# A decoder layer on one core: the ACT and Vector instructions of a transposed block in another order, and another start of the first product

## The chip, the cores and the metric

The kernel runs on one core of a Trainium2 chip. The metric is device time in microseconds (us) of one execution, with all loads and stores. Lower is better. In what follows PE is the tensor engine (matmuls and transposes), ACT the scalar engine, DVE the vector engine, SP the engine whose queue issues most DMAs.

## The reference, cut to what matters

One layer of a decoder over 256 tokens (two halves `m` of 128) with 2048 channels in float32: a normalised input goes through a wide product, two attention branches, an output product, an MLP with squared ReLU, and a gated embedding at the end.

```python
u = rmsnorm(h, g_mix_pre)                       # 256 x 2048
proj = u @ w_in                                 # 2048 x 10240: q, k, v of both branches, two gates
oa, ob = moba_attention(...), diff_attention(...)
mixed = sigmoid(ga) * (oa @ w_br_moba) + sigmoid(gb) * (ob @ w_br_diff)
h = h + rmsnorm(mixed @ w_out, g_mix_post)
u2 = rmsnorm(h, g_mlp_pre)
h = h + rmsnorm(square(relu(u2 @ w_up)) @ w_down, g_mlp_post)
gate = sigmoid(rmsnorm(h, g_ple_pre) @ w_ple_gate)
h = h + rmsnorm((p @ w_ple_proj) * gate, g_ple_post)
```

## The kernel before, in words

Every product is a row of chunks of 512 output columns (`Chunk`, `run`). A chunk of 16 k-tiles is done in 8 pieces `s` of two k-tiles (512 KB of weights), each for the two token halves `m`. A float32 product is built from three matmuls on halves of the numbers: weights are split into `whi` (an ACT copy, `head`, L227) and `wlo` (a DVE subtraction, `low`, L234), the moving side likewise into `hi` and `lo`. So one piece for one half is two times (L294 with `whi` and the high part of u, L295 with `wlo` and the high part, L296 with `whi` and the low part of u), six matmuls of 512 columns.

The order is written by hand: each engine runs its instructions in program order, and the waits between engines are put in by the layer that the kernel is written in, from what each instruction reads and writes. `ensure(i)` emits the splitting of weights up to piece `i`; `heads` and `low` feed ACT and DVE. Raw weights have 5 buffers, split ones 8. SP loads raw piece `i` when the DVE subtraction of piece `i - 5` is done.

Three times the left side of a product is made from rows in SBUF: u from x in the first product, u2 and u3 from h at two boundaries (after the output product, and after the last down product). A block is 128 tokens by 512 channels. `turn` (L173) makes four PE transposes into one PSUM bank; `turned` (L180) scales them by the norm's gain while copying them out: for each of four columns of 128, one ACT instruction writes the high part (L189) and one DVE instruction the low part (L190, it reads the same bank and the high part). With a gain there are 8 blocks at each of the three places, 24 in all, 96 pairs of instructions.

In the first product a hook, `first`, places that work: the x blocks of the next four k-tiles are transposed at the hook of `(s, 1)` for even `s`, ahead of that piece's matmuls, and `turned` at the hook of the next odd `s`. Before it stands the start (L613 to L637): DMAs, idle matmuls on zeros (`warm`), the gain's transpose, the first block and the first piece of weights, which is split in two halves of one k-tile.

At a boundary the class `Boundary` (L717) places, in a list, turns `T(m, kg)`, scalings `U(m, kg)`, the residual additions `A(m, kg)` on DVE (L746) that make h, and single weight splits `H(s)` on ACT and `L(s)` on DVE, among two short products (`pp_ch`) and the next product.

Of the kernel before, what the change touches and what calls it, by code (L numbers as in the profile page):

```python
# [11 lines left out]
F32 = mybir.dt.float32  # L12
F32R = mybir.dt.float32r
I32 = mybir.dt.int32
AF = mybir.ActivationFunctionType
ALU = mybir.AluOpType
# [3 lines left out]
P = 128  # L20
# [10 lines left out]
CW = 512  # L31
KT = 2
# [4 lines left out]
NB = 8  # L37
# [42 lines left out]
def tile_hybrid_block(ctx: ExitStack, tc: tile.TileContext, a, out: bass.AP):  # L80
    nc = tc.nc
    pe, act, dve = nc.tensor, nc.scalar, nc.vector
# [7 lines left out]
    wp = ctx.enter_context(tc.tile_pool(name="wp", bufs=1))  # L90
# [5 lines left out]
    def aux(name):  # L96
        return ps.tile([P, 512], F32, name=name, tag="aux", bufs=4)
# [5 lines left out]
    gT = [cst.tile([P, NT], F32, name=f"gT{i}") for i in range(3)]  # L103
# [7 lines left out]
    def load_small():  # L111
        for i, g in ((1, "g_mlp_pre"), (2, "g_ple_pre")):
            nc.sync.dma_start(gr[i], a[g][0].rearrange("(k p) -> k p", p=P))
        nc.sync.dma_start(con[:, P:C_END], a["consts"][:, P:C_END])
        for i, n in enumerate(("lambda_q1", "lambda_k1", "lambda_q2", "lambda_k2")):
            nc.sync.dma_start(lamv[:, i, :], a[n][0:1, :].to_broadcast([P, HD]))
        nc.sync.dma_start(gsub, a["diff_subln_g"][0:1, :].to_broadcast([P, 2 * HD]))

    def setup_gain(i):
        g_ps = aux("g_ps")  # L120
        pe.transpose(g_ps[:, 0:NT], gr[i], ident[0:NT, 0:NT])
        dve.tensor_copy(gT[i], g_ps[:, 0:NT])
# [14 lines left out]
    def rstd(ss, n, out_ap, tag, rest=None):  # L137


        w = ss.shape[-1]  # L140
        v = sm.tile([P, w], F32, name="v", tag=f"v{tag}", bufs=2)
        dve.tensor_scalar(v, ss, -0.5 / n, -0.5 * EPS if rest is None else rest, op0=ALU.mult, op1=ALU.add)
        y = sm.tile([P, w], F32, name="y", tag=f"y{tag}", bufs=2)
        dve.tensor_scalar(y.bitcast(I32), v.bitcast(I32), -0.5, 519526879.0, op0=ALU.mult, op1=ALU.add)
        t = sm.tile([P, w], F32, name="t", tag=f"t{tag}", bufs=2)
        for i in range(3):
            if w == 1:
                dve.tensor_scalar(t, v, y, y, op0=ALU.mult, op1=ALU.mult)
            else:
                dve.tensor_mul(t, y, y)  # L150
                dve.tensor_mul(t, t, v)
            dve.scalar_tensor_tensor(out_ap if i == 2 else y, t, 1.5, y, op0=ALU.add, op1=ALU.mult)
# [16 lines left out]
    def split(hi, lo, src):  # L169
        act.activation(hi, src, AF.Copy)  # L170
        dve.tensor_sub(lo, src, hi.bitcast(F32))

    def turn(src):  # L173

        t_ps = aux("t_ps")
        for j in range(4):
            pe.transpose(t_ps[:, j * P:(j + 1) * P], src[:, j * P:(j + 1) * P], ident)
        return t_ps.rearrange("p (j t) -> p j t", j=4)

    def turned(t_ps, dst, kg, m, gain=None, js=range(4)):  # L180

        s = slice(m * P, (m + 1) * P)
        if gain is None:
            split(dst.hi[kg][:, :, s], dst.lo[kg][:, :, s], t_ps)
            return
        for j in js:
            g = gT[gain][:, 4 * kg + j:4 * kg + j + 1]
            hi = dst.hi[kg][:, j, s]
            act.activation(hi, t_ps[:, j], AF.Copy, scale=g)  # L189
            dve.scalar_tensor_tensor(dst.lo[kg][:, j, s], t_ps[:, j], g, hi.bitcast(F32), op0=ALU.mult, op1=ALU.subtract)  # L190


    chunks = []
# [1 line left out]
    conv = {}  # L195
# [3 lines left out]
    raws = {}  # L199
# [12 lines left out]
    def loads(i):  # L212
        while state["load"] <= i:
            load(state["load"])

    def head(i):

        c, s = todo[i]
        kts = c.subs[s]
        n = len(kts)  # L220
        loads(i)
        raw = raws.pop(i)
        cuts = [slice(j, j + 1) for j in range(n)] if i < 2 else [slice(0, n)]
        hi = wp.tile([P, KT, CW], F32R, name="whi", tag="whi", bufs=NB)
        lo = wp.tile([P, KT, CW], F32R, name="wlo", tag="wlo", bufs=NB)
        for j in cuts:
            act.activation(hi[:, j], raw[:, j], AF.Copy)  # L227
        conv[i] = (hi, lo, raw, cuts)

    def low(i):  # L230

        hi, lo, raw, cuts = conv[i]
        for j in cuts:
            dve.tensor_sub(lo[:, j], raw[:, j], hi[:, j].bitcast(F32))  # L234
        conv[i] = (hi, lo)

    def heads(i):
        last = min(i, state["used"] + NB - 1, len(todo) - 1)
        while state["head"] <= last:
            head(state["head"])  # L240
            state["head"] += 1

    def ensure(i):
        last = min(i, state["used"] + NB - 1, len(todo) - 1)
        while state["conv"] <= last:
            heads(state["conv"])
            low(state["conv"])
            state["conv"] += 1
# [89 lines left out]
    uT = Tbuf("A", "u")  # L338
    oT = Tbuf("B", "o")
    x_sb = [gp.tile([P, 2, 2, CW], F32, name=f"x{i}", tag="xg", bufs=2) for i in range(2)]  # L340
# [43 lines left out]
    def attention(u):  # L384
# [101 lines left out]
        for m in range(2):  # L486
            t_ps = turn(ob[:, m].rearrange("p h d -> p (h d)"))
            yield
            turned(t_ps, oT, u, m)
# [24 lines left out]
    def mix(n):  # L514
        for _ in range(3):
            yield
        for m in range(2):
            t_ps = turn(G[n][:, 1, m, :])
            yield
            turned(t_ps, mT, n, m)  # L520

    all_kt = list(range(NT))
    c_in = []
# [6 lines left out]
    for tag, u, kind, col in seq:  # L530
# [4 lines left out]
        c = Chunk(w_in, all_kt, col, uT)  # L535
# [3 lines left out]
    for n in range(4):  # L539
        for wh in range(2):  # L540
            c = Chunk(w_in, all_kt, 6144 + 2048 * wh + n * CW, uT)
# [3 lines left out]
    for n in range(4):  # L545
        for wh in range(2):
            c = Chunk(w_bm if wh == 0 else w_bd, list(range(8)), n * CW, None)
# [37 lines left out]
    def load_x(kg):  # L585
        nc.sync.dma_start(x_sb[kg // 2][:, kg % 2], x_d[:, kg * CW:(kg + 1) * CW].rearrange("(m p) c -> p m c", p=P))

    xt = {}

    def first(s, m):  # L590
        kg = (s + 1) // 2
        if (s, m) == (0, 1):
            xt[1] = turn(x_sb[0][:, 0, 1])
            turned(xt[1], uT, 0, 1, 0)
        if s % 2 == 0:
            if m and kg < 3:
                xt.update({mm: turn(x_sb[(kg + 1) // 2][:, (kg + 1) % 2, mm]) for mm in range(2)})
            if m and kg < 2:
                load_x(kg + 2)
        elif kg < 4 and m == 0:  # L600
            for mm in range(2):
                turned(xt[mm], uT, kg, mm, 0)
        for k, mm in {3: ((0, m),), 5: ((1, m),), 6: ((2, m),), 7: ((3, 0), (3, 1)) if m == 0 else ()}.get(s, ()):
            junk = at.tile([P, CW], F32, name="junk", tag="t1", bufs=1)
            act.activation(junk, x_sb[k // 2][:, k % 2, mm], AF.Square, accum_out=ss1[:, mm, k:k + 1])
        if (s, m) == (5, 1):
            load_small()
        if (s, m) == (7, 0):
            ss1t = sm.tile([P, 2], F32, name="ss1t", bufs=1)
            dve.tensor_reduce(ss1t, ss1, AX.X, ALU.add)  # L610
            rstd(ss1t, D, rs1, "x")
# [4 lines left out]
    def warm(n):  # L616
        w = aux("warm")
        for i in range(n):
            pe.matmul(w[:, 0:P], lhsT=z, rhs=z, start=True, stop=True)
# [4 lines left out]
    nc.scalar.dma_start(x_sb[0][:, 0, 1], x_d[P:T, 0:CW])  # L624
    loads(2)
    load_x(1)
    warm(8)
    setup_gain(0)
    warm(2)
    xt[0] = turn(x_sb[0][:, 0, 0])  # L630
    head(0)
    turned(xt[0], uT, 0, 0, 0, range(2))
    low(0)
    turned(xt[0], uT, 0, 0, 0, range(2, 4))
    state["head"] = state["conv"] = 1
    c_in[0].hook = first
    c_in[0].ahead = lambda s, m: (2 * m, 2, 2, 2, 2, 2, 4, 5)[s]  # L637

    for c in order1:
# [242 lines left out]
    for g in range(4):  # L882
        hT = Tbuf("A", f"h{g}")
        for n in range(4):
            c = up_ch[4 * g + n]
# [13 lines left out]
        for n in range(4):  # L899
            c = dn_ch[g][n]  # L900
# [89 lines left out]
```

## Time and profile before

| | |
|---|---|
| median of 3 runs | 1524.48 us (1522.71 to 1524.62) |
| profiled execution: time, span | 1523.25 us, 1521.5 us |
| PE busy | 1488.4 us, 98% |
| DVE busy | 866.7 us, 57% |
| ACT busy | 716.5 us, 47% |
| DMA | 185 GB/s over the span, queue q1 57% of 16 engines |
| mean granted clock of PE | 0.99 of full |

The span is the time from the first to the last instruction; the 1.75 us beside it lie around it. Busy shares are means over stages with different limits. The rows below are from several views of the same execution: `idle before` and `<-` name the wait of an engine and what ended it.

### The profile page before, as it was taken

To read this page: it belongs to the slowest core of one execution; us is meant where nothing else is said; L and a number is where in the kernel's file an instruction comes from. 1 tells how busy PE (TensorE), PEld (TensorE's weight loads), DVE (VectorE), ACT (ScalarE), POOL (GpSimd) and SP (SyncE) were. 2 spreads that over 40 slices of the span, in tenths; PEclk is the share of its full clock that TensorE was granted. 3 is DMA by queue.
4 is the path that set the end of the run, shared out by engine and by line. 5 is a ranking of instruction groups with operands and counts; after the bars stand their busy time and mean duration, and the time that the engine had idled before them with its cause. 6 is when DMAs were issued, how large, how long until landed. Compare 5 with 4: busy or idle time off the path is not lost.

```text
span 1521.5 us, 18536 instructions
## 1 busy us (share of the span) xinstructions
PE 1488.4 (98%) x7119; PEld 1245.1 (82%) x7119; DVE 866.7 (57%) x1111; ACT 716.5 (47%) x995; POOL 0.2 (0%) x4
## 2 busy tenths in 40 slices
PE   8999999999999999998999999999999999999897
PEld 6788888888888888886888888888888888888686
DVE  4755555655344565556664456545655555655675
ACT  5654444554544444445554444433544344543662
POOL 0000000000000000000000000000000000000000
PEclk9999999999999999999999999999999999999999
DMA  7655555555466556744656564666456646565272
GB/s 228 222 188 163 182 157 177 167 177 183 153 221 207 180 187 221 250 138 149 211 180 201 187 207 157 208 204 194 156 190 217 194 149 214 182 205 201 68 247 94
DMA packets 146537, 282.14 MB, mean 185 GB/s; under 512 B 8928, under 2 KB 10896, under 8 KB 146192
## 3 DMA queue, kind: packets, MB, share of 16 engines
q1 hardware_dynamic: 145984, 280.28, 57.0%
q8 instruction: 56, 0.92, 0.2%
q10 hardware_dynamic: 464, 0.66, 0.1%
q14 instruction: 33, 0.27, 0.1%
HBM read 278.81 MB, written 2.10 MB: 185 GB/s over the span
## 4 chain that ended last, share of the span: by engine, by line
PE 91%; DVE 4%; ACT 3%; DMA 1%; issue 1%; SPq 0%; DVEq 0%; ACTq 0%
PE acc L295 22%; PE acc L296 22%; PE acc L294 22%; PE acct L322 15%; PE acct L323 7%; DVE u L190 2%; ACT u L189 2%; DVE wlo L234 1%; ACT whi L227 1%; DVE h L746 1%; PE s_ps L397 1%; DMA raw<-in_w_in 1%; PE acc L950 0%; PE acc L952 0%; PE acc L951 0%
## 5 line engine op out<-in xcount | busy, mean ns | idle before, releaser
L234 DVE TENSOR_TENSOR wlo<-raw,whi 128x1024 fp32r<-128x1024 f32 (+1 forms) x518 | 617.7, 1219 | 423.3 <-ACT whi L227 422.6
L227 ACT ACTIVATE whi<-raw 128x1024 fp32r<-128x1024 f32 (+1 forms) x518 | 531.4, 1051 | 406.6 <-PE acc L296 283.7
L322 PE MATMUL acct<-u,whi 128*128 128x512 f32 x960 | 338.4, 397 | 1.0 <-ACT r L827 1.0
L294 PE MATMUL acc<-whi,u 128*128 128x512 f32 x768 | 309.3, 403 | 5.5 <-ACT whi L227 4.8
L295 PE MATMUL acc<-wlo,u 128*128 128x512 f32 x768 | 302.6, 394 | 5.3 <-DVE wlo L234 5.3
L296 PE MATMUL acc<-whi,u 128*128 128x512 f32 x768 | 302.5, 394 | 0.0
L323 PE MATMUL acct<-u,wlo 128*128 128x256 f32 x960 | 269.4, 281 | 0.0
L322 PEld LDWEIGHTS acct<-u,whi 128*128 128x128 f32 x960 | 180.2, 188 | 45.2 <-ACT r L827 1.4
L295 PE MATMUL acc<-wlo,h 128*128 128x512 f32 x512 | 199.2, 389 | 0.0
L294 PE MATMUL acc<-whi,h 128*128 128x512 f32 x512 | 199.2, 389 | 0.0
L296 PE MATMUL acc<-whi,h 128*128 128x512 f32 x512 | 199.2, 389 | 0.0
L323 PEld LDWEIGHTS acct<-u,wlo 128*128 128x128 f32 x960 | 181.4, 189 | 0.2
L294 PEld LDWEIGHTS acc<-whi,u 128*128 128x128 f32 x768 | 146.3, 190 | 37.1 <-ACT whi L227 7.3
L295 PEld LDWEIGHTS acc<-wlo,u 128*128 128x128 f32 x768 | 146.0, 190 | 36.3 <-DVE wlo L234 7.5
L296 PEld LDWEIGHTS acc<-whi,u 128*128 128x128 f32 x768 | 145.8, 190 | 30.9
L294 PEld LDWEIGHTS acc<-whi,h 128*128 128x128 f32 x512 | 96.1, 188 | 20.1
L296 PEld LDWEIGHTS acc<-whi,h 128*128 128x128 f32 x512 | 96.1, 188 | 19.9
L295 PEld LDWEIGHTS acc<-wlo,h 128*128 128x128 f32 x512 | 96.1, 188 | 19.8
L844 ACT ACTIVATE r<-acct 128x256 f32<-128x256 f32 x60 | 22.8, 379 | 67.7 <-PE acct L323 67.7
L189 ACT ACTIVATE u<-t_ps,gT 128x128 fp32r<-128x128 f32 x96 | 34.0, 366 | 43.9 <-DVE u L190 42.4
L190 DVE SCALAR_TENSOR_TENSOR u<-t_ps,gT,u 128x128 fp32r<-128x128 f32 x96 | 32.8, 349 | 36.6 <-ACT u L189 36.6
L845 DVE TENSOR_TENSOR r<-acct,r 128x256 f32<-128x256 f32 x60 | 24.5, 422 | 47.2 <-ACT r L844 47.2
(160 smaller groups left out, 1041.4 us busy)
## 6 DMA issues: line engine op xcount, KB each, us to landing
raw<-in_w_in SPq DMA_DIRECT2D x159, 512.0 KB, 4.2
raw<-in_w_up SPq DMA_DIRECT2D x128, 512.0 KB, 4.2
raw<-in_w_down SPq DMA_DIRECT2D x128, 512.0 KB, 5.3
raw<-in_w_out SPq DMA_DIRECT2D x32, 512.0 KB, 5.2
raw<-in_w_ple_gate SPq DMA_DIRECT2D x32, 512.0 KB, 5.4
raw<-in_w_br_moba SPq DMA_DIRECT2D x16, 512.0 KB, 3.9
raw<-in_w_br_diff SPq DMA_DIRECT2D x16, 512.0 KB, 4.9
h<-in_x SPq DMA_DIRECT2D x2, 1024.0 KB, 10.1
```

What stands on the lines that cost most here:

```text
L189: act.activation(hi, t_ps[:, j], AF.Copy, scale=g)
L190: dve.scalar_tensor_tensor(dst.lo[kg][:, j, s], t_ps[:, j], g, hi.bitcast(F32), op0=ALU.mult, op1=ALU.subtract)
L227: act.activation(hi[:, j], raw[:, j], AF.Copy)
L234: dve.tensor_sub(lo[:, j], raw[:, j], hi[:, j].bitcast(F32))
L294: pe.matmul(acc[m], lhsT=ah, rhs=hi[:, j, :], start=first, stop=False)
L295: pe.matmul(acc[m], lhsT=ah, rhs=lo[:, j, :], start=False, stop=False)
L296: pe.matmul(acc[m], lhsT=al, rhs=hi[:, j, :], start=False, stop=last)
L322: pe.matmul(acc[q].rearrange("p a t -> p (a t)"), lhsT=hi[:, j, ws], rhs=mv, start=first, stop=False)
L323: pe.matmul(acc[q][:, 0], lhsT=lo[:, j, ws], rhs=mv[:, 0:T], start=False, stop=last)
L397: pe.matmul(s_ps[:, j, :], lhsT=q[:, h, m * P:(m + 1) * P], rhs=k[:, h, 0:w], start=True, stop=True)
L844: act.activation(r[:, q % 2], acc[:, 1], AF.Copy)
L845: dve.tensor_add(r[:, q % 2], acc[:, 0], r[:, q % 2])
```

## The change

`turned` with a gain first issues its ACT instructions (up to four), then its DVE instructions. At the start there are 4 and 1 idle matmuls in place of 8 and 2, and the first piece of weights and the first block are interleaved by halves: split half 0 of the weights on ACT and DVE, scale two columns, then the same for half 1. In the first product the transposes of the next x blocks move from ahead of the matmuls of `(s, 1)` to behind them (`script` runs after a piece's matmuls). `head` and `low` get a parameter for the halves, and otherwise do what they did.

```diff
+        g = [gT[gain][:, 4 * kg + j:4 * kg + j + 1] for j in range(4)]
         for j in js:
-            g = gT[gain][:, 4 * kg + j:4 * kg + j + 1]
-            hi = dst.hi[kg][:, j, s]
-            act.activation(hi, t_ps[:, j], AF.Copy, scale=g)
-            dve.scalar_tensor_tensor(dst.lo[kg][:, j, s], t_ps[:, j], g, hi.bitcast(F32), op0=ALU.mult, op1=ALU.subtract)
+            act.activation(dst.hi[kg][:, j, s], t_ps[:, j], AF.Copy, scale=g[j])
+        for j in js:
+            dve.scalar_tensor_tensor(dst.lo[kg][:, j, s], t_ps[:, j], g[j], dst.hi[kg][:, j, s].bitcast(F32),
+                                     op0=ALU.mult, op1=ALU.subtract)
...
+    def turn_x(kg):
+        xt.update({mm: turn(x_sb[kg // 2][:, kg % 2, mm]) for mm in range(2)})
+
     def first(s, m):
...
         if s % 2 == 0:
-            if m and kg < 3:
-                xt.update({mm: turn(x_sb[(kg + 1) // 2][:, (kg + 1) % 2, mm]) for mm in range(2)})
             if m and kg < 2:
                 load_x(kg + 2)
...
-    warm(8)
+    warm(4)
     setup_gain(0)
-    warm(2)
+    warm(1)
     xt[0] = turn(x_sb[0][:, 0, 0])
-    head(0)
-    turned(xt[0], uT, 0, 0, 0, range(2))
-    low(0)
-    turned(xt[0], uT, 0, 0, 0, range(2, 4))
+    for j in range(2):
+        head(0, j)
+        low(0, j)
+        turned(xt[0], uT, 0, 0, 0, range(2 * j, 2 * j + 2))
     state["head"] = state["conv"] = 1
     c_in[0].hook = first
+    c_in[0].script = {(2 * g, 1): [lambda g=g: turn_x(g + 1)] for g in range(3)}
```

## Rows read from the trace of the kernel before

**Rows 1.** Busy time by stretch of the span: length, PE, PEld, DVE, ACT, POOL, granted clock, DMA share, GB/s
```profile
0.00:50.00 50.00, 40.80 (x160) 31.35 (x161) 25.50 (x55) 29.88 (x64) 0.20 (x4) 0.90 0.67 212
50.00:670.00 620.00, 620.00 (x2835) 515.00 (x2834) 345.25 (x420) 295.03 (x392) 0.00 (x0) 1.00 0.60 191
670.00:730.00 60.00, 53.85 (x259) 43.96 (x258) 40.50 (x77) 35.97 (x76) 0.00 (x0) 0.94 0.39 128
...
1400.00:1450.00 50.00, 42.45 (x189) 34.01 (x188) 32.31 (x72) 29.51 (x67) 0.00 (x0) 0.93 0.27 86
```
**Rows 2.** What PE waited for, 670 to 730 us: total, times, longest
```profile
PE t_ps L177 <- DVE h L746: 3.7, 1, 3.7
...
PE acc L295 <- DVE wlo L234: 0.8, 1, 0.8
PE acc L294 <- ACT whi L227: 0.6, 1, 0.6
```
**Rows 3.** The same view, 1400 to 1450 us, its longest wait
```profile
PE t_ps L177 <- DVE h L746: 6.1, 1, 6.1
```
**Rows 4.** Groups of instructions, whole span: busy, mean ns | idle before, releaser
```profile
L234 DVE TENSOR_TENSOR wlo<-raw,whi 128x1024 fp32r<-128x1024 f32 (+1 forms) x518 | 617.7, 1219 | 423.3 <-ACT whi L227 422.6
L227 ACT ACTIVATE whi<-raw 128x1024 fp32r<-128x1024 f32 (+1 forms) x518 | 531.4, 1051 | 406.6 <-PE acc L296 283.7
...
L189 ACT ACTIVATE u<-t_ps,gT 128x128 fp32r<-128x128 f32 x96 | 34.0, 366 | 43.9 <-DVE u L190 42.4
L190 DVE SCALAR_TENSOR_TENSOR u<-t_ps,gT,u 128x128 fp32r<-128x128 f32 x96 | 32.8, 349 | 36.6 <-ACT u L189 36.6
```
**Rows 5.** Who waited for line L190, whole span: us, times
```profile
  PEld t_ps L177: 1.1, 2
```
**Rows 6.** Timeline of the first product, ACT and DVE: start, us, instruction, idle before
```profile
13.86 0.37 ACT L189 ACTIVATE u<-t_ps,gT 128x128 fp32r<-128x128 f32 x1 [0.42 <-DVE u L190]
...
20.13 0.62 ACT L189 ACTIVATE u<-t_ps,gT 128x128 fp32r<-128x128 f32 x2 [0.42 <-DVE u L190]
...
20.53 0.61 DVE L190 SCALAR_TENSOR_TENSOR u<-t_ps,gT,u 128x128 fp32r<-128x128 f32 x2 [0.43 <-ACT u L189]
```
**Rows 7.** Timeline of the first product, PE: where it went on after a wait, and its end
```profile
9.58 0.50 PE L295 MATMUL acc<-wlo,u 128*128 128x512 f32 x1 [1.28 <-DVE wlo L234]
...
11.19 2.76 PE L177 MATMUL t_ps<-con,x 128*128 128x128 f32 x12
...
15.58 0.50 PE L294 MATMUL acc<-whi,u 128*128 128x512 f32 x1 [0.22 <-ACT whi L227]
...
24.11 0.50 PE L294 MATMUL acc<-whi,u 128*128 128x512 f32 x1 [1.38 <-ACT whi L227]
...
42.13 0.49 PE L294 MATMUL acc<-whi,u 128*128 128x512 f32 x1 [0.87 <-ACT whi L227]
...
47.40 0.39 PE L121 MATMUL g_ps<-con,gr 16*128 16x16 f32 x2
```
**Rows 8.** Timeline, PE: transposes of x at the start, and later
```profile
5.99 1.06 PE L177 MATMUL t_ps<-con,x 128*128 128x128 f32 x4
...
20.30 1.04 PE L177 MATMUL t_ps<-con,x 128*128 128x128 f32 x8
```
**Rows 9.** Chain that ended last: steps of one matmul near the first product's end
```profile
45.34 0.43 PE acc L295
...
49.26 0.23 PE acc L296
```
**Rows 10.** Busy time of one us (columns as in Rows 1) behind the wait at 24 us
```profile
25.00:26.00 1.00, 0.63 (x3) 0.54 (x4) 1.00 (x2) 0.26 (x2) 0.00 (x0) 1.00 0.43 68
```
**Rows 11.** Timeline of the first boundary: first scaling, first addition of h, transposes
```profile
678.88 0.36 ACT L189 ACTIVATE u<-t_ps,gT 128x128 fp32r<-128x128 f32 x1
...
686.74 1.41 DVE L746 SCALAR_TENSOR_TENSOR h<-og,r,h 128x512 f32<-128x512 f32 x2
...
687.54 1.12 PE L177 MATMUL t_ps<-con,h 128*128 128x128 f32 x4 [3.70 <-DVE h L746]
```

More of the change, by code (lines that the diff above doesn't have):

```diff
@@ L214, in loads, with head, low @@
             load(state["load"])
-    def head(i):
+    def head(i, cut=None):
         c, s = todo[i]
-        kts = c.subs[s]
-        n = len(kts)
+        n = len(c.subs[s])
         loads(i)
[L222 to L226, printed above, removed]
+        if cut in (None, 0):
+            hi = wp.tile([P, KT, CW], F32R, name="whi", tag="whi", bufs=NB)
+            lo = wp.tile([P, KT, CW], F32R, name="wlo", tag="wlo", bufs=NB)
+            conv[i] = (hi, lo, raws.pop(i), [slice(j, j + 1) for j in range(n)] if i < 2 else [slice(0, n)])
+        hi, lo, raw, cuts = conv[i]
+        for j in cuts if cut is None else cuts[cut:cut + 1]:
             act.activation(hi[:, j], raw[:, j], AF.Copy)
-        conv[i] = (hi, lo, raw, cuts)
-    def low(i):
+    def low(i, cut=None):
         hi, lo, raw, cuts = conv[i]
-        for j in cuts:
+        for j in cuts if cut is None else cuts[cut:cut + 1]:
             dve.tensor_sub(lo[:, j], raw[:, j], hi[:, j].bitcast(F32))
-        conv[i] = (hi, lo)
+        if cut in (None, len(cuts) - 1):
+            conv[i] = (hi, lo)
     def heads(i):
```

## The prediction

> **What bounds the kernel now.** I read the busy time by stretches first. Between the first product and the first boundary PE is busy for 620.0 of 620 us at full clock [rows 1]; the stretch from 730 to 1400 us looks the same. There nothing but less PE work would help, and the change removes none. So the time it can touch lies in three stretches, where PE stands idle for 9.2, 6.2 and 7.6 us and the granted clock is 0.90, 0.94 and 0.93 [rows 1]. What PE waits for there is DVE and ACT work: at the two boundaries the addition of h, 3.7 and 6.1 us in one wait each [rows 2, 3], in the first product the split weights [rows 7].
>
> The groups of instructions then show why ACT and DVE are late although they are busy for half the span only. The 96 ACT scalings take 34.0 us, and ACT idles 42.4 us just before them for the DVE instruction of the same block; DVE idles 36.6 us for ACT [rows 4]. The next ACT scaling needs nothing that this DVE instruction writes. Both read one PSUM bank, and the rows fit an order that is kept between the engines on a bank as the program gives it, readers too. So the two alternate: 0.37 and 0.42 us of waiting in one step [rows 6], 0.79 us for each of the 96 pairs, and neither engine does anything else meanwhile, because its queue is in order. A block holds both for 4 x 0.79 = 3.15 us. Where two scalings stand side by side, at the seam of two blocks, two take 0.62 us on ACT and two take 0.61 us on DVE [rows 6]: a further one costs 0.26 us.
>
> **Part 1: scalings first.** In the new order ACT does its four in 0.37 + 3 x 0.26 = 1.15 us, and DVE, which must now wait for the last of the four, its own in 1.13 us. A block goes from 3.15 to 2.3 us in latency, and from 3.15 to about 1.05 us of each engine's queue. The first low part comes 0.78 us later than before, the last 0.85 us earlier. Two blocks in a row overlap, for they lie in two banks (DVE starts at 20.53 while ACT's second scaling of 20.13, the next block's, still runs [rows 6]).
>
> *First product.* From piece 1 on, the work repeats every two pieces: (1,0) goes on at 15.58, (7,0) at 42.13 [rows 7], three cycles of 8.85 us. ACT's queue explains one: 8 alternations of 0.79 (6.3 us) and two weight heads of 1.05 [rows 4] are 8.4 us. New: ACT has 8 x 0.26 + 2 x 1.05 = 4.2 us, up to 5.8 with two statistics of about 0.8; DVE has 8 x 0.26 + 2 x 1.22 = 4.5 us. PE needs 24 matmuls of 0.23 [rows 9] and 8 transposes in 1.04 [rows 8], 6.56 us, and becomes the bound: 3 x (8.85 - 6.56) = 6.9 us. The last piece took 42.13 to 47.40 with two waits and half of it at the 0.43 us step; 12 x 0.23 = 2.76 saves 2.5 us.
>
> *Boundaries.* From the first scaling at 678.88 to the first addition of the second half at 686.74 DVE's queue holds two blocks and one `wlo` [rows 11]. New: ACT's first block ends at 680.0, DVE's 1.05 us of it lie beside the weight head that ACT does next, ACT's second block runs from 680.9 to 682.0, DVE's until 683.1, `wlo` adds 1.13, so h comes at about 684.2, 2.5 us earlier. PE's wait of 3.7 becomes 1.2. Behind the long wait PE ran at half clock; 0.06 x 60 = 3.6 us is all that the clock cost in that stretch [rows 1], and some of it lies in the wait itself. A wait of 1.38 us in the first product was followed by full clock [rows 7, 10], so I take this gone, 2.4 us. The waits of 0.6 and 0.8 us for the first weights behind the transposed blocks [rows 2] go as well: the last four blocks there alternate without anything between, and their DVE work shrinks by 2 us a block, more than PE's own gain. With the transposes' wait for a block's low part, half of 1.1 [rows 5], the first boundary gives 2.5 + 2.4 + 1.4 + 0.5 = 6.8 us. At the second the same queue gives 2.5 of 6.1 us, 3.6 remain, about as long as the wait that halved the clock at the first, so I count no clock: 2.5 + 1.4 + 0.5 = 4.4 us. If the clock stays up there, 2.4 more; if it falls at the first, 2.4 less.
>
> **Part 2: the start.** Piece (0,0) waited 1.28 us for `wlo`, which stood behind two alternations, and the transposes after it began at 11.19 [rows 7]. With the half-wise order they begin at 9.3 to 9.9. The x blocks now stand behind piece (0,1), which needs its own block's four scalings and first low part, 9.9 + 0.3 + 1.15 + 0.35, thus 11.7, then 4 more matmuls and 8 transposes (1.04 at full clock, 1.7 at half). So (1,0) starts between 13.4 and 15.5, before it was 15.58. I take 1.5 us; bounds 0 and 2.2. The five idle matmuls stand ahead of the first x, whose DMA sets the start, so they return nothing themselves. What they may cost is the clock: at most the 0.43 against 0.23 us step [rows 9] for as long as it stays low, 0.2 us a matmul. In the kernel before, too, PE ran at half clock from the end of (0,0) on (12 transposes in 2.76 us against 8 in 1.04) [rows 7, 8], so I count a loss only in the bound: 18 matmuls of the first pieces, 3.6 us.
>
> The trace bears on this once more: the transposes at 5.99 go at 0.21 to 0.27 us each, those at 20.30 at 0.13 [rows 8], so the idle matmuls had not yet brought the full clock. The Trainium skill (TensorE: Matmul & The Clock Gate, Part 1) says that the clock is throttled by default and that activity releases it; the trace agrees, and the rule speaks against taking idle matmuls out. By it the first pieces would all run at the low level, which is the bound just given and the first rival below.
>
> **Part 3: transposes behind the piece.** Same count on PE. Each pair of blocks is ready for ACT one piece-half (1.4 us) later. From the transposes' end to the first use lie 12 matmuls, 2.75 us; the first block's low parts need 2.3, the second's 3.4 but 1.4 later. That fits by 0.5 to 0.7 us, so I take nothing. SP's queue keeps its order, and its buffers come free earlier; POOL has no part in it.
>
> **Sum.** 1.5 + 6.9 + 2.5 = 10.9 for the first product, 6.8 and 4.4 for the boundaries: 22.1 us. The profiled execution, 1523.25 us, would come to 1501.2; it lies 1.2 us below the median, so against the median of 1524.48 I predict 1502.4 us.
>
> **Rivals.** (1) *Cold start.* PE's low clock lasts through the first pieces: 18 to 40 matmuls at 0.2 us, 3.6 to 8 us less: 1506 to 1510. For it: rows 8 and the gaps while x lands; against it: once fed, PE came back to full clock within a few us each time. (2) *ACT or the late blocks take the bound.* The margin of part 3 is used up by the statistics and heads in front of a block; 2 us at each of three block pairs: 1508.5. Against it: ACT has 5.8 of 6.56 us. (3) *The alternation stays,* because it does not come from the order of the code but from some other wait: only the start's 1.5 us remain, 1523. Against it: the seams of rows 6. (4) *Slower.* The thin start leaves PE below full clock for good, not for pieces: the gain of 22.1 us is used up by 110 matmuls at 0.2 us, more than the first product has (96). If both of the first two products ran so, 192 x 0.2 = 38 us: 1541. For it speaks only the clock of 0.90 in rows 1; against it that full clock returned before 49.26 [rows 9] while ACT and DVE fed worse.
>
> **Numbers.** Forecast 0.75, rival (1) 0.08, (2) 0.08, (3) 0.05, (4) 0.04. Lower end: 11.6 for the first product (start at 2.2), 8.0 at the first boundary (its last 1.2 us of waiting gone too), 6.8 at the second with its clock kept, and the 1 us by which runs differ: 1497. Upper end: rivals (1) and (2) in their middle, or 8 + 4.4 + 3.5: 1509. About 0.2% (3 us) is what a measurement can tell here from no change: faster 0.92, same 0.04 (most of rival 3), slower 0.04.
>
> **What would show it.** Four ACT scalings in a row 0.26 us apart, and ACT's idle time before them down from 42.4 to a few us; the g_ps transposes at about 36.5 in place of 47.40; cycles of 6.6 us with PE without waits in between; PE's waits for h near 1.2 and 3.6 us and no wait for weights behind the blocks; the stretches between unchanged. Wrong would be: DVE waits that put the 0.78 us of the first low part on PE; a clock of 0.5 beyond 15 us; a wait for h as long as before.

## The result, and the profile after

The changed kernel takes 1496.71 us (median of 4 runs, 1494.97 to 1499.79), the kernel before 1524.55 beside it (4 runs, 1522.71 to 1525.25): a ratio of 0.9821 [0.9801, 0.9842], 27.8 us less. The forecast was 1502.4 us, 22.1 less, with a range from 1497 to 1509. So the direction and the order of size came as forecast, the gain was 5.7 us larger, and the median lies 0.3 us under the range. The profiled execution of the changed kernel is its slowest, 1499.79 us (span 1497.9). It is 23.5 us shorter than the profiled execution of before; the other 4.4 us are that this one lies 3.1 us above its median and the one of before 1.3 below.

First the busy time by stretches, of the changed kernel (length; then busy time of PE, PEld, DVE, ACT, POOL; granted clock, DMA share, GB/s), as in [rows 1]:

```profile
0.00:50.00 50.00, 46.51 (x199) 36.98 (x200) 32.17 (x75) 33.59 (x72) 0.20 (x4) 1.00 0.75 247
50.00:670.00 620.00, 620.00 (x2835) 514.77 (x2834) 343.75 (x424) 293.88 (x396) 0.00 (x0) 1.00 0.59 189
670.00:730.00 60.00, 58.84 (x319) 50.11 (x318) 46.62 (x84) 40.91 (x79) 0.00 (x0) 1.00 0.55 179
...
1400.00:1450.00 50.00, 50.00 (x223) 41.39 (x222) 35.89 (x62) 32.83 (x60) 0.00 (x0) 0.98 0.61 201
```

PE's idle time went from 9.2 to 3.5 us at the start and from 6.2 to 1.2 at the first boundary, and is nothing in the last stretch, out of which the second boundary's transposes have moved (they now start at 1396.63). The long stretch is busy for 620 of 620 us, as before.

The groups of the transposed blocks' two instructions, the changed kernel (busy, mean ns | idle before, and its releasers), against [rows 4]:

```profile
L188 ACT ACTIVATE u<-t_ps,gT 128x128 fp32r<-128x128 f32 x96 | 27.6, 401 | 14.5 <-PE t_ps L177 14.3 <-DVE u L190 0.2
L190 DVE SCALAR_TENSOR_TENSOR u<-t_ps,gT,u 128x128 fp32r<-128x128 f32 x96 | 26.3, 338 | 11.2 <-ACT u L188 11.1
```

The releaser has changed: ACT's 42.4 us of waiting for DVE have become 0.2, and what is left, 14.3, is for PE, which now is the one that others wait for. DVE still waits for ACT, once a block and not once an instruction: 11.1 us where it was 36.6.

The timeline of the changed kernel (start, us, instruction; in brackets the idle time before it):

```profile
9.30 0.63 PE L296 MATMUL acc<-wlo,u 128*128 128x512 f32 x1
9.73 0.63 PE L297 MATMUL acc<-whi,u 128*128 128x512 f32 x1
...
15.80 2.18 ACT L188 ACTIVATE u<-t_ps,gT 128x128 fp32r<-128x128 f32 x8 [1.43 <-PE t_ps L177]
16.26 0.61 PE L295 MATMUL acc<-whi,u 128*128 128x512 f32 x1
16.97 2.16 DVE L190 SCALAR_TENSOR_TENSOR u<-t_ps,gT,u 128x128 fp32r<-128x128 f32 x8 [1.09 <-ACT u L188]
...
22.76 0.47 PE L295 MATMUL acc<-whi,u 128*128 128x512 f32 x1
...
28.33 1.03 PE L177 MATMUL t_ps<-con,x 128*128 128x128 f32 x8
29.12 0.48 PE L295 MATMUL acc<-whi,u 128*128 128x512 f32 x1
...
34.68 0.39 PE L295 MATMUL acc<-whi,u 128*128 128x512 f32 x1
...
37.49 0.29 PE L121 MATMUL g_ps<-con,gr 16*128 16x16 f32 x2
...
668.76 1.14 ACT L188 ACTIVATE u<-t_ps,gT 128x128 fp32r<-128x128 f32 x4
...
674.88 0.66 PE L177 MATMUL t_ps<-con,h 128*128 128x128 f32 x4 [1.16 <-DVE h L749]
...
697.21 0.39 PE L323 MATMUL acct<-u,whi 128*128 128x512 f32 x1
...
1396.63 1.12 PE L177 MATMUL t_ps<-con,h 128*128 128x128 f32 x4 [3.33 <-DVE h L749]
...
1398.40 0.63 PE L297 MATMUL acc<-whi,u 128*128 128x512 f32 x1
1398.83 0.63 PE L295 MATMUL acc<-whi,u 128*128 128x512 f32 x1
```

Eight scalings, two blocks, take 2.18 us on ACT and eight Vector instructions 2.16 us on DVE, 1.17 us behind; two blocks took 8 x 0.79 = 6.3 us before. From (1,0) at 16.26 over (3,0) at 22.76 and (5,0) at 29.12 to (7,0) at 34.68 PE goes on without a wait. The product ends at 37.49 where it was 47.40 [rows 7]. At the first boundary the wait is 1.16 us and the four transposes behind it take 0.66 us in place of 1.12 [rows 11]: the clock stayed up. At the second the wait is 3.33 us, and behind it matmuls follow each other in 0.43 us, the low level of the clock (1.2 of 2.4 GHz): the step of a matmul is 0.43 us at that level and 0.23 us at full clock [rows 9]. The same 0.43 us stand at 9.30 to 9.73, at the start.

### The profile page after: what moved, and what is told of

The parts are those of the page before. It is cut to its first block, busy times and chain, and to the rows that moved or that the text cites. A ratio compares the mean times of both kernels' runs of the same rounds, so it can differ in the third digit from the quotient of the medians.

```text
span 1497.9 us, 18528 instructions
## 1 busy us (share of the span) xinstructions
PE 1479.8 (99%) x7109; PEld 1240.0 (83%) x7109; DVE 860.6 (57%) x1111; ACT 710.9 (47%) x995; POOL 0.2 (0%) x4
## 4 chain that ended last, share of the span: by engine, by line
PE 97%; DVE 1%; ACT 1%; DMA 0%; issue 0%; SPq 0%; DVEq 0%; ACTq 0%
PE acc L295 23%; PE acc L297 23%; PE acc L296 23%; PE acct L323 15%; PE acct L324 8%; PE t_ps L177 1%; PE s_ps L398 1%; PE acc L953 0%; PE acc L955 0%; PE acc L954 0%; PE qk_ps L366 0%; ACT u L188 0%; DVE h L749 0%; DMA x<-in_x 0%; PE o_ps L457 0%; PE o_ps L471 0%
## 5 line engine op out<-in xcount | busy, mean ns | idle before, releaser
L295 PE MATMUL acc<-whi,o 128*128 128x512 f32 x128 | 50.4, 394 | 0.0
L295 PE MATMUL acc<-whi,m 128*128 128x512 f32 x128 | 50.1, 391 | 0.0
```

Of the source, the lines that this page charges most:

```text
L295: pe.matmul(acc[m], lhsT=ah, rhs=hi[:, j, :], start=first, stop=False)
```

## The experiments

The theory: the gain comes from the order of ACT and DVE on one PSUM bank, which the program's order sets; grouped scalings alone bring nearly all of it. The difference between the executions is PE's clock at the start and at the second boundary. The rivals are named at each run. Times are medians; ratios are to the kernel before, run beside them.

**The changed kernel again** (no edit). Is 1496.7 the kernel's time, and what makes it spread over 4.8 us?

> The changed kernel once more, for its spread and for the clock at the start. Theory: its profiled execution (1499.79 us) ran matmuls at the 0.43 us step from 7.4 to 16.2 us; that stretch and the one behind the wait at the second boundary differ between executions, so executions spread over 1495 to 1500 us and the shortest have the higher mean clock. Rival: the spread has nothing to do with the clock; then mean clocks don't order the times.

1497.13 us (1495.24 to 1499.99), ratio 0.9823 [0.9809, 0.9836], 26.6 us less. The profiled execution took 1495.24 us. Its timeline:

```profile
14.65 0.48 PE L295 MATMUL acc<-whi,u 128*128 128x512 f32 x1
...
35.73 0.29 PE L121 MATMUL g_ps<-con,gr 16*128 16x16 f32 x2
...
1394.89 0.66 PE L177 MATMUL t_ps<-con,h 128*128 128x128 f32 x4 [3.35 <-DVE h L749]
```

This and the execution above are one program. Here the low clock of the start ends at about 11 and not at 16.2 us, and the first product ends 1.76 us earlier; behind the same wait at the second boundary, 3.35 us, the four transposes take 0.66 us, and 2.7 us are saved by 1402. Together that is the 4.5 us between the two. So the clock after these waits is not the same in each execution, and what the prediction could foresee is an interval of 4.5 us, not a point in it. The mean granted clocks of the four runs fit: 0.997 at 1495.24 us, 0.996 and 0.997 at 1497.10 and 1497.16, 0.995 at 1499.99.

**The scalings alone** (the kernel before with the first block of the change's diff, the new loop of `turned`, and nothing else of the change).

> The kernel before with only the scalings regrouped (four on ACT, then four on Vector). Theory: this is most of the change: cycles of two pieces in the first product fall from 8.85 to about 6.6 us, PE's waits for h from 3.7 and 6.1 to 1.2 and 3.4 us, in all 20 to 24 us less than before. Rival (the start's edits carry it): at most 13 us less.

1498.59 us (1497.80 to 1499.00), ratio 0.983 [0.9817, 0.9843]: 25.1 of the 26.6 us, a little above the 20 to 24 expected. The first product ends at 36.78, and PE's two waits for h are those of the full change:

```profile
PE t_ps L177 <- DVE h L747: 4.5, 2, 3.4
```

**The start alone** (the changed kernel with the old loop of `turned`, that block of the diff undone).

> The changed kernel with the scalings alternating again, so only the idle matmuls, the halves at the start and the moved transposes are new. Theory: boundaries as before (waits 3.7 and 6.1 us), cycles still near 8.8 us, 0 to 3 us less than before. Rival (the start's edits carry it): 8 us less or more.

1522.33 us (11 runs, 1520.76 to 1523.51), ratio 0.9989 [0.998, 0.9998]: 1.4 us. The two parts add up, 25.1 + 1.4 = 26.5. ACT waits for DVE as before:

```profile
L189 ACT ACTIVATE u<-t_ps,gT 128x128 fp32r<-128x128 f32 x96 | 34.1, 367 | 43.6 <-DVE u L190 41.6 <-PE t_ps L177 1.9
```

In this profile the wait at the first boundary was 3.72 us, as long as the 3.70 of before [rows 2]. The transposes behind it still ran at full clock, and 0.7 us after their start the clock fell (PE's timeline, then the busy time of one us with the columns of [rows 1], the granted clock at 0.50):

```profile
685.40 0.66 PE L177 MATMUL t_ps<-con,h 128*128 128x128 f32 x4 [3.72 <-DVE h L748]
685.81 0.50 PE L294 MATMUL acc<-whi,u 128*128 128x512 f32 x1
686.12 0.61 PE L295 MATMUL acc<-wlo,u 128*128 128x512 f32 x1
686.53 0.63 PE L296 MATMUL acc<-whi,u 128*128 128x512 f32 x1
...
687.00:688.00 1.00, 1.00 (x4) 0.81 (x3) 0.40 (x2) 0.49 (x2) 0.00 (x0) 0.50 0.75 289
```

**The idle matmuls back** (the changed kernel, `warm(4)` to `warm(8)` and `warm(1)` to `warm(2)`, as before the change). It tells whether fewer idle matmuls cause the low clock of the start.

> The changed kernel with 8 and 2 idle matmuls as before. Theory (thin start leaves PE at the low clock): the first matmuls, from about 7.8 us, step at 0.23 us, no stretch at 0.43 until 16 us, and the first product ends 1 to 2 us earlier than in the changed kernel. Rival (the idle matmuls had no use, and x sets the start): the 0.43 us stretch is there too, and the end is the same within 0.3 us or later.

1497.15 us (1495.20 to 1500.05), ratio 0.982 [0.9806, 0.9834]: no difference. Its timeline:

```profile
7.21 0.50 PE L295 MATMUL acc<-whi,u 128*128 128x512 f32 x1 [0.46 <-ACT u L188]
7.56 0.39 PE L296 MATMUL acc<-wlo,u 128*128 128x512 f32 x1
...
8.84 0.51 PE L295 MATMUL acc<-whi,u 128*128 128x512 f32 x1 [0.48 <-ACT whi L228]
9.56 0.66 PE L296 MATMUL acc<-wlo,u 128*128 128x512 f32 x1 [0.22 <-DVE wlo L234]
10.03 0.63 PE L297 MATMUL acc<-whi,u 128*128 128x512 f32 x1
...
37.66 0.29 PE L121 MATMUL g_ps<-con,gr 16*128 16x16 f32 x2
```

The first matmuls do run at full clock, but they then wait for the split weights, 0.48 and 0.22 us by this view with more gaps that it doesn't put down to anyone, and from 9.56 on the steps are those of the low level again. The product ends at 37.66. So in this execution the idle matmuls ahead of x buy speed for instructions whose operands are late anyway, and lose it again. By the medians, leaving five of them out cost nothing.

**Two blocks interleaved** (the kernel before; in the first product alone the two blocks of a pair go together, one column of each at a time; in the second cut loop stands the Vector instruction):

```diff
+    def turned_pair(t, dst, kg, gain):
+        for j in range(4):
...
+            for m in range(2):
+                act.activation(dst.hi[kg][:, j, m * P:(m + 1) * P], t[m][:, j], AF.Copy, scale=g)
+            for m in range(2):
...
-            for mm in range(2):
-                turned(xt[mm], uT, kg, mm, 0)
+            turned_pair(xt, uT, kg, 0)
```

Within one bank the engines still take turns. If what costs the time is any handshake between ACT and DVE, it stays; if it is an order kept for each bank, one block works while the other waits.

> The kernel before; in the first product the two blocks of a pair (two PSUM banks) are scaled in turns: ACT on block A, ACT on block B, Vector on A, Vector on B, column by column, so each bank still sees ACT and Vector alternate. Theory (the order is kept per bank): a pair takes about 3.2 to 3.6 us in place of 6.3, cycles fall from 8.8 to about 6.6 us, the first product ends near 38 to 40 us in place of 47.4, 7 to 10 us less than before; boundaries unchanged. Rival (the handshake is between the engines whatever the bank): a pair still takes 6.3 us and the time is that of before within 2 us.

1515.81 us (1515.47 to 1516.26), ratio 0.9943 [0.9929, 0.9956]: 9.3 us less. Between the two profiled executions the span is 7.4 us shorter, and 6.8 of it is the first product, which ends at 40.58 (expected 38 to 40); the waits at the boundaries, where nothing was edited, are the old ones. Its timeline:

```profile
20.07 0.63 ACT L197 ACTIVATE u<-t_ps,gT 128x128 fp32r<-128x128 f32 x2 [1.04 <-DVE u L200]
20.48 0.61 DVE L200 SCALAR_TENSOR_TENSOR u<-t_ps,gT,u 128x128 fp32r<-128x128 f32 x2 [0.18 <-ACT u L197]
20.86 0.63 ACT L197 ACTIVATE u<-t_ps,gT 128x128 fp32r<-128x128 f32 x2 [0.16 <-DVE u L200]
21.26 0.61 DVE L200 SCALAR_TENSOR_TENSOR u<-t_ps,gT,u 128x128 fp32r<-128x128 f32 x2 [0.18 <-ACT u L197]
```

The period is 0.79 us as in [rows 6], but it now carries two pairs and not one: a pair of blocks takes 3.2 us in place of 6.3. ACT's next instruction on the first block starts at 20.86, while DVE's pair that began at 20.48 still works on the second block. So the rival, a handshake of the engines whatever they read, falls, and so does an order kept on the buffer that both blocks write, for they share it (`dst.hi[kg]`). What is left is an order on the bank, or on the block in it: a block fills one bank, so no run here tells these two apart. The Trainium skill (PSUM — Partial Sum Buffer, section "PSUM bank collisions raise a hardware error") says that the compiler adds a dependency between any two instructions on different engines that touch the same bank (and the same 32-partition quadrant), two readers included. By this rule two banks are free of each other, and the trace agrees: 3.2 against 6.3 us. Which program put these waits in, no run here shows.

**The transposes of x ahead of the piece again** (the changed kernel without part 3 of the change: `turn_x(kg + 1)` stands before the second half of an even piece, and the entry for it in the script goes).

> The changed kernel with the x transposes back ahead of the matmuls of (s,1). Theory: with the scalings regrouped PE is the bound of the cycles either way, so only the wait for x in the first piece differs, 0 to 1 us slower than the changed kernel. Rival (blocks behind the piece are late and cost PE waits): faster than the changed kernel by 1 us or more.

1496.94 us (1494.56 to 1499.31), ratio 0.9819 [0.9806, 0.9832]: the same as the changed kernel. Its profiled execution ends the first product at 35.04. The part is worth nothing that can be measured.

**The clock held at the second boundary** (the changed kernel; ten idle matmuls go into the bank ahead of the transposes that wait for h):

```diff
+        for _ in range(idle):
+            pe.matmul(t_ps[:, 0:P], lhsT=z2, rhs=z2, start=True, stop=True)
...
+                idle = (0 if self.gain == 1 else 10) if (m, kg) == (1, 0) else 0
```

> The changed kernel with 10 idle matmuls on zeros ahead of the first transposes of the second half at the second boundary, in PE's wait of 3.3 us there. Theory (that wait sometimes drops PE to half clock, at 2.5 to 2.7 us): matmuls behind it step at 0.23 us in every execution, the slow group of times near 1498 to 1500 goes; the median 1 to 2 us under the changed kernel's, never above. Rival (the clock at that place has nothing to do with the wait): the spread stays as it is.

1497.01 us (1495.40 to 1497.08), ratio 0.9817 [0.9804, 0.983]. Its timeline:

```profile
1393.09 2.39 PE L180 MATMUL t_ps<-z 128*128 128x128 f32 x20
1396.61 0.66 PE L182 MATMUL t_ps<-con,h 128*128 128x128 f32 x4 [1.13 <-DVE h L754]
```

The records show two per matmul. They fill 2.39 us, 1.13 of the wait are left, and the clock stays up: 0.66 us. None of the four runs is near 1500 us, and the spread is 1.7 us and not 4.8 (four runs are few to show this), but the lower median that was expected didn't come. The profiled execution has the long low clock at the start (its first product ends at 37.46). This fits a spread with two sources, of which the edit takes away one.

**The addition of h earlier** (the changed kernel; at both boundaries the additions of the second half move ahead of the scalings and low parts that needn't come first; A is an addition, U a block's scalings, T its transposes, H and L a weight's high and low part):

```diff
-            pps[0].script = {(0, 0): [T(0, 0)], (0, 1): [T(0, 1), U(0, 0), H(4), U(0, 1)]}
-            pps[1].script = {(0, 0): [T(0, 2), L(3), A(1, 0), A(1, 1), U(0, 2)],
-                             (0, 1): [T(0, 3), H(5), L(4), A(1, 2), A(1, 3), U(0, 3), L(5)]}
+            pps[0].script = {(0, 0): [T(0, 0)], (0, 1): [T(0, 1), U(0, 0), A(1, 0), H(4), U(0, 1)]}
+            pps[1].script = {(0, 0): [T(0, 2), A(1, 1), L(3), U(0, 2)],
+                             (0, 1): [T(0, 3), H(5), A(1, 2), L(4), A(1, 3), U(0, 3), L(5)]}
```

> The changed kernel with the additions of the second half ahead of the weight splits on Vector at both boundaries (first addition right behind the first block). Theory (PE's wait for h is Vector's queue): the waits of 1.2 and 3.3 us shrink to under 0.5 and about 1, some 0.5 to 1 us of it comes back as waits for a later weight split or block; 1.5 to 3 us less than the changed kernel, up to 2.7 more where the clock had fallen. Rival (the queue only moves its wait): the sum of PE's waits at the boundaries stays at 4.5 us.

1493.54 us (1493.14 to 1493.94), ratio 0.9797 [0.9783, 0.981], 3.2 to 3.6 us under the changed kernel. PE's waits behind the boundaries (us in total, times, longest):

```profile
PE t_ps L177 <- DVE h L749: 1.0, 2, 0.8
PE t_ps L177 <- DVE u L190: 1.0, 2, 0.8
```

4.5 us of waiting for h have become 1.0 for h and 1.0 for DVE's scalings of the blocks, in four pieces, the longest 0.8, and the clock didn't fall at a boundary in the profile. So 2.5 us of the gain are shorter waits; that the rest is the clock is argued. What the change left there was an order on DVE's queue, not DVE's work.

**The start filled** (on top of the last: idle matmuls behind each early group, so that PE doesn't stand still while the first split weights come), and that last kernel again beside it:

```diff
             turned(xt[1], uT, 0, 1, 0)
+            warm(4)
...
     setup_gain(0)
+    warm(4)
...
+        if j == 2:
+            for _ in range(2):
+                pe.matmul(t_ps[:, 2 * P:3 * P], lhsT=z, rhs=z, start=True, stop=True)
...
     warm(1)
-    xt[0] = turn(x_sb[0][:, 0, 0])
```

> The kernel with the earlier additions, and idle matmuls in the gaps of the start: 4 in place of 1 ahead of the first transposes, 2 between their halves, 1 behind them, 4 behind the transposes of the second half's first block. Theory (gaps of PE at the start let the low clock last into the first pieces, 11 to 16 us, worth 1 to 2.5 us by the spread of the first product's end between executions): no matmul of the first product at the 0.43 us step, its end at 34.5 to 35.5 us in place of 35.7 to 37.5, 0.5 to 2 us less than with the earlier additions alone. Rival (the clock at the start is set by something else, or the idle matmuls are in the way): still 0.43 us steps, the same time or up to 1 us more.

> The changed kernel with the earlier additions once more, on the same chip as the filled start. Theory: 1493.5 us within 1 us; PE's waits at the boundaries 2.0 us in all, the first product ends between 35.5 and 37.5 us by its clock.

With the start filled 1492.44 us (1492.10 to 1492.71), ratio 0.9789 [0.9776, 0.9803]; without it 1493.41 (1493.14 to 1495.13), 0.9797 [0.9783, 0.981]. Timeline of the first:

```profile
7.31 0.50 PE L295 MATMUL acc<-whi,u 128*128 128x512 f32 x1 [0.23 <-ACT u L188]
7.65 0.40 PE L296 MATMUL acc<-wlo,u 128*128 128x512 f32 x1
...
34.49 0.29 PE L121 MATMUL g_ps<-con,gr 16*128 16x16 f32 x2
```

and of the second:

```profile
37.34 0.29 PE L121 MATMUL g_ps<-con,gr 16*128 16x16 f32 x2
```

With the gaps filled no matmul of the first product runs at the low level, and in these two executions the product ends 2.9 us earlier; by the medians 1.0 us is left of it. The low clock of the unfilled start lasts long in some executions and short in others (in the first profile of the same kernel, 1493.59 us, the product ended at 35.99), which would account for the smaller difference. The ranges of the two don't overlap. This is the fastest version of all, 31.8 us under the kernel before.

## Why the prediction was right, and where its sizes were off

**The mechanism** (two engines taking turns on one bank) is shown: undone alone it loses 25 of 26.6 us, done alone it gains them, and two banks free the engines from each other. The rates were as forecast too: 0.26 us a further instruction, four in 1.14 us (forecast 1.15). ACT's idle time before the scalings fell to 14.5 us and not to a few, but only 0.2 of it is for DVE; the rest is for PE, which the prediction had as the new bound without counting ACT's wait for it.

**First product:** 9.9 us in the profiled execution, 11.7 in the second one, forecast 10.9. Of the three terms:
- *The cycles*, forecast 3 x (8.85 - 6.56) = 6.9 us, gave 26.55 - 18.42 = 8.1 (from 16.26 to 34.68). PE became the bound, as said. The step undersized it twice: the eight transposes delay the next matmul by 0.79 us (28.33 to 29.12), not by their busy time of 1.04, and the third cycle has none.
- *The last piece*, forecast 2.5: 5.27 - 2.81 = 2.5.
- *The start*, forecast 1.5 with bounds 0 and 2.2: (1,0) began at 16.26, 0.7 us later than before, and at 14.65, 0.9 earlier, in the other execution. This step failed in the profiled one, and lay outside its bounds: the low clock lasted until 16.2 us. The prediction names a loss of up to 3.6 us for that, but its bounds of 0 and 2.2 don't hold it, and by its own sign (a low clock beyond 15 us) it was wrong here. Where the low clock ended early it was 0.9 us, still not 1.5. The first matmul on the low part started at 12.83 in both executions, forecast 11.7: the transposes of the block began at 10.2 to 10.3, not by 9.9, and the first scaling came 1.0 to 1.1 us behind that, not 0.3.

**First boundary:** forecast 6.8 us, measured 8.7 (the first scaling came 10.1 us earlier than before, that of the second boundary 18.8). The queue's 2.5 us are 2.54 (678.88 to 687.54 is 8.66 us, 668.76 to 674.88 is 6.12), the wait is 1.16 us (forecast 1.2), the clock stays up. It came as forecast, but the reason given was one wait of 1.38 us that full clock had followed. The next cycle of the same trace shows the other case, behind waits of 1.13 us (at 32.91) and 0.76 us (PE's timeline of the kernel before, then one us with the granted clock at 0.50):

```profile
34.17 0.67 PE L295 MATMUL acc<-wlo,u 128*128 128x512 f32 x1 [0.76 <-DVE wlo L234]
34.63 0.63 PE L296 MATMUL acc<-whi,u 128*128 128x512 f32 x1
...
35.00:36.00 1.00, 1.00 (x4) 0.74 (x3) 0.93 (x2) 0.03 (x1) 0.00 (x0) 0.50 0.72 152
```

From the transposes behind h to the first matmul into `acct` (714.71 before, 697.21 now) the kernel gained 4.84 us where the prediction had 2.4 + 1.4 + 0.5 = 4.3; the remaining 1.3 us come later, and hold a wait of 1.04 us for `r`, an ACT result of the next product, which the prediction had not listed and which is gone. So the mis-sized term is the stretch behind the blocks. That waits further on went with the backlog of ACT and DVE is argued from these rows; no run separates it.

**Second boundary:** forecast 4.4 us without the clock, measured 4.8 in the execution in which the clock fell. The wait is 3.33 us (forecast 3.6). In the executions in which it stays up it is 2.7 us more (forecast "2.4 more"). The prediction argued from the 3.70 us at the first boundary that the wait of 3.6 us left here halves the clock. Behind 3.70 to 3.72 us the clock did fall in all three profiles that have such a wait: at once in the kernel before, 0.7 us later in the run with the start alone, and about 1 us later with two blocks interleaved. Behind the slightly shorter wait that came, the runs show both: behind 3.33 us here it fell, behind 3.35 us in the second execution it did not. So this value could not be chosen, and it was luck that the profiled execution had the one that was.

**From these to the medians.** Cycles, last piece and start 9.9, 0.2 between, 8.7 and 4.8 make 23.6 us between the two profiled spans. A typical run of the changed kernel then has one of the two clock losses (1.8 and 2.7 us) less. That a median run lies between them fits the five profiles that show both places (with the low clock long at the start and fallen at the second boundary 1499.79 and 1499.78 us, with neither 1495.24 and 1494.56, with the start's alone 1497.08 in the run with the clock held); of the runs without a profile it is argued, not shown. The lower end of the range had the gains of both clocks in it, but not the larger cycles and the wait for `r`.

**Parts 2 and 3.** The five idle matmuls cost nothing (1497.15 with them back), as the sum had it; the transposes behind the piece bring nothing (1496.94 without), as forecast.

**The rivals.** *Cold start:* the low clock at the start is there, from 7.4 to 16.2 us, but it costs 1.8 us over its short form (37.49 against 35.73) and 2.9 us over none (37.34 against 34.49 with the start filled), not 3.6 to 8. With the five idle matmuls back it begins later, at 9.6, but the product ends no earlier. *ACT or the late blocks:* no PE wait of that kind stands in the cycles. *The alternation stays:* ACT's wait for DVE is 0.2 us; the run with the start alone shows what this rival would have been, 1522.33 us (its price was 1523). *Slower:* the clock was back at 16.3 us, and the steps of the rest of the first product are 0.23 us.

## What to carry to other kernels

Where two engines read one PSUM bank, look at the releaser column of their groups: if each names the other in turn, write all instructions of the one engine ahead of those of the other, or let two banks alternate; here that was worth 25 of 1524 us without touching the amount of work. Then read again what the queue of the late engine holds ahead of the value that the bottleneck waits for, for moving the additions there gave another 3.2 to 3.6 us. Give a forecast that rests on the clock behind a wait as two values, and don't choose one from a single execution.

## What was not expected of the hardware

The column of the granted clock doesn't show the start. In the changed kernel it reads 1.00 in a stretch in which the matmuls follow each other at 0.43 us, 9.30 to 9.73 in the timeline above; this is the microsecond from 9 to 10 (columns as in [rows 1]):

```profile
9.00:10.00 1.00, 1.00 (x4) 0.77 (x3) 0.58 (x2) 0.00 (x0) 0.00 (x0) 1.00 1.06 412
```

With the start filled the same microsecond has no such steps, at nearly the same DMA rate (406 GB/s), so the transfers are not what makes them. The mean that this view gives for the first 50 us, 1.00, is too high for the same reason; the step between two matmuls of one shape tells the level there.

PE's waits for h at the boundaries and the level behind them, over the profiled executions: behind 1.16 us full in all six; behind 3.33 to 3.35 us low in three (the changed kernel, the scalings alone, the idle matmuls back) and full in two (the changed kernel again, the transposes ahead); behind 3.70 to 3.72 us low in all three, in two of them only 0.7 to 1 us after the wait; behind 6.08 to 6.09 us (the second boundary of the kernel before, the start alone, two blocks interleaved) low in all three. So the first instruction behind a wait doesn't tell the level; the next microsecond has to be read too. What decides between the two levels behind 3.33 to 3.35 us, no run here shows.
